# First down product: when the weight sums are formed and when the residual is read back

## The chip, the cores and the metric

The kernel runs on one core of a Trainium2 chip. The metric is the device time of one execution in microseconds (us), the median of several runs. The kernel's program is fixed at build time: each engine (PE for matmuls, ACT, DVE, POOL, and SP, which here only issues DMAs) has its own list of instructions, runs it strictly in order, and waits on semaphores where an operand or a buffer isn't ready. DMAs are issued by SP (plain loads and stores) and by POOL (transfers from memory to memory that can also add into their destination). Both kinds are carried by the same 16 DMA engines.

## The reference

One macaron layer on 512 tokens of width 1024, all in float32. The change touches only the end of the first of its three parts:

```
x = x + 0.5 * swiglu_ffn(rmsnorm(x, ffn1_norm), ffn1_w_gate, ffn1_w_up, ffn1_w_down)
x = x + hybrid_mixer(rmsnorm(x, mix_norm), ...)
x = x + 0.5 * swiglu_ffn(rmsnorm(x, ffn2_norm), ffn2_w_gate, ffn2_w_up, ffn2_w_down)
x = rmsnorm(x, final_norm)

swiglu_ffn(x, g, u, d) = (silu(x @ g) * (x @ u)) @ d      # g, u: 1024 x 2816, d: 2816 x 1024
```

## The kernel before

Each float32 product is made of three faster passes (`mm3`): an operand is split into a high part (rounded, ACT, `whi` for weights and `ah` for activations) and a low part (the remainder, DVE, `wlo`), and high x high, high x low and low x high are added up in PSUM. So each block of weights is loaded by a DMA into a tile `raw`, cast by ACT, subtracted by DVE, and only then multiplied.

Both feed-forward parts multiply by a Strassen-like scheme (Winograd's form, seven block products in place of eight). It needs sums of weight blocks. The gate and up weights are summed on DVE while they are in the chip. The sums of the four blocks of the down weights (B11, B12, B21, B22) are formed in memory: T1 = B11 + B12, T2 = T1 + B22, T3 = B12 + B22, T4 = T2 + B21 (signs are left to the other operand), each cut into G = 6 groups of rows (the last one half as wide), stored in DRAM tiles named `wsum`. For each of these 24 tiles there are two DMAs from POOL: one copies the first term into it, the other adds the second term to it (`accum_op`). These 48 steps are listed in `Down.steps`; those of one tile, and those that build on another tile, must land in order, and POOL waits for a landing where the next step reads or adds to the same tile.

The order in time of the first feed-forward part:

1. `ffn_up`, the up product, some 220 us. Its loop over blocks of 128 hidden columns (`for n in range(PLAIN, KF)`, 17 blocks, about 10 us each) fetches two blocks ahead (`fetch`, L436 and L437: two DMAs of 512 KB into one of two `raw` tiles), casts (`high` and `low`, L444 and L449), and multiplies. Once a block, and three times before the loop, it calls `down.make_sums(..., 2)`: POOL copies one column of a fresh tile (`mark`, L673, which ties POOL to that point of the program) and issues the next two of the 48 steps (L675). That is 20 calls, so 40 steps.
2. The first three of the seven products of the down part: for each of the six groups T2, B11 and T1 (`Down.product`: load L702 by `fetch`, cast and subtract L131 and L132 by `split`, then 12 matmuls, 6 for the last group). The block stands under `tc.manual_schedule(engines={SP})`: SP issues in the order in which the program is written. `product` issues one more step of the weight sums at every second product from the seventh on; that is where the last eight of the 48 go.
3. The other four products (T3 and B22 in turn, then B21, then T4). This block stands under the scheduler, which may move DMAs of SP ahead of others where it believes that they can start. From the 20th product on, each `product` also issues one of eight loads of the residual (`down.loads`, L760: 256 KB of the layer's input each, into the tiles `x`, which hold blocks of activations, `xa`, up to the end of the up product). The result is transposed and added to `x` (`add`, L835), and the second norm follows.

There are four `raw` tiles for the loads of the down part (two of the up product's and two of the weights' pool) and four pairs of tiles for their high and low parts, used in strict rotation. So SP can issue a load when the DVE is done with the load four products back, and the casts run at most four products ahead of PE.

Of the kernel before, what the change touches and what calls it, by code (L numbers as in the profile page):

```python
# [11 lines left out]
AF = mybir.ActivationFunctionType  # L12
ALU = mybir.AluOpType
# [3 lines left out]
P = 128  # L17
D = 1024
S = 512
KD = D // P  # L20
NT = S // P
FF = 2816
KF = FF // P
KH = KF // 2
# [15 lines left out]
PLAIN = 5  # L40
# [13 lines left out]
def layer(  # L54
# [31 lines left out]
    nc = tc.nc  # L86
# [14 lines left out]
    def name(what):  # L101
        n_tiles[0] += 1
        return f"{what}_{n_tiles[0]}"

    def temp(dtype=F32):
        return tpool.tile([P, S], dtype, tag="t", name=name("t"))

    def bank(tag="mm", bufs=4):
        return ps.tile([P, S], F32, tag=tag, name=name(tag), bufs=bufs)

    def abank():
        return bank("a", 4)
# [3 lines left out]
    B11, B12, B21, B22, T1, T2, T3, T4 = range(8)  # L116
    A11, S1, S3, S2, A12, A22, S4 = range(7)
# [4 lines left out]
    def piece(n=1):  # L122
        for _ in range(min(n, len(todo))):
            what, *args = todo.pop(0)
            what(*args)


    def split(src, hi, lo, scale=None):

        if scale is None:  # L130
            nc.scalar.copy(hi, src)  # L131
            nc.vector.tensor_tensor(lo, src, hi.bitcast(F32), op=ALU.subtract)  # L132
        else:
            nc.scalar.activation(hi, src, AF.Copy, scale=scale)
            nc.vector.scalar_tensor_tensor(
                lo, src, scale, hi.bitcast(F32), op0=ALU.mult, op1=ALU.subtract
            )
# [48 lines left out]
    def residual_tiles():  # L186
        pairs = [xpool.tile([P, 2 * S], F32, tag=f"x{k}", name=name("x")) for k in range(KD // 2)]
        return [pairs[k // 2][:, k % 2 * S : (k % 2 + 1) * S] for k in range(KD)]

    x = residual_tiles()  # L190
# [4 lines left out]
    ident = const.tile([P, P], F32, name="ident")  # L195
# [70 lines left out]
    class Norm:  # L266


        def __init__(self, which):
            self.which, self.h, self.acc = which, {}, None  # L270

        def add(self, k, square=True):
            hi = hpool.tile([P, S], F32R, tag="h", name=name("hhi"))
            lo = hpool.tile([P, S], F32R, tag="h", name=name("hlo"))
            split(x[k], hi, lo, gain_sb[:, self.which, k : k + 1])
            self.h[k] = hi, lo
            if square:
                self.square(k)
# [41 lines left out]
        def blocks(self, pool, aside):  # L320
# [43 lines left out]
            def extra():  # L364
                return pool.tile([P, 4 * HT], F32R, tag="extra", name=name("sa"), bufs=2)

            free = [3, 2, 1, 0]
            return [(scale, k) for k in range(KD)] + [
                (add, s1, a21, a22, ALU.subtract),
                (add, s2, s1, a11, ALU.add),  # L370
                (add, a21, a11, a21, ALU.add),
                (whole, S3, a21, by_x(free), -1.0),
                (whole, S2, s2, by_x(free), -1.0),
# [244 lines left out]
    G = len(groups)  # L618

    class Down:  # L620
# [11 lines left out]

        def __init__(self, order, pair, block):

            self.order, self.pair, self.block = order, pair, block

            self.terms = {T1: (B11, B12), T2: (T1, B22), T3: (B12, B22), T4: (T2, B21)}
            self.wsum = {  # L640
                (i, g): dram.tile(list(block(B11, g).shape), F32, name=name("wsum"))
                for i in self.terms for g in range(G)
            }

            self.steps = sorted(
                (g + at + 2 * (i - T1), at, i, g)
                for i in self.terms for g in range(G) for at in range(2)
            )
# [18 lines left out]

        def make_sums(self, after, n):

            part, self.steps[:n] = self.steps[:n], []  # L670
            with tc.manual_schedule(engines={mybir.EngineType.Pool}):
                mark = small.tile([P, 1], F32, tag="mark", name=name("mark"))
                nc.gpsimd.tensor_copy(mark, after[:, 0:1])  # L673
                for _, at, i, g in part:
                    nc.gpsimd.dma_start(  # L675
                        self.rows(i, g), self.rows(self.terms[i][at], g),
                        **(dict(accum_op=ALU.add) if at else {}),
                    )
# [86 lines left out]
    def whole(make):  # L765
        return [[(make(), 0, S)] for _ in range(2)]

    def scaled(dst, acc, scale, other, op=ALU.add):
        nc.vector.scalar_tensor_tensor(dst, acc, scale, other, op0=ALU.mult, op1=op)

    def halved(acc):
        z = [temp() for _ in range(2)]
        for tt in range(2):
            nc.scalar.activation(z[tt], acc[tt][0][0], AF.Copy, scale=0.5)
        return z


    n1, n2, n3 = Norm(0), Norm(1), Norm(2)
# [15 lines left out]

    KPS = (2, 3, 0, 1)
    order1 = [0, 1, KH, KH + 1] + [f + KH * j for f in range(2, KH) for j in range(2)]
    down1 = Down(order1, lambda f: (f % KH, f // KH), block1)
    down2 = Down(list(range(KF)), lambda f: (f // 2, f % 2), block2)

    with tc.tile_pool(name="act1", bufs=1, reuse_waits="tile") as apool:  # L800
        down1.begin(apool)
        ffn_up(n1, wA1, down1, loaded=False)
        p1, p5, p6 = whole(bank), whole(bank), whole(abank)

        with tc.manual_schedule(engines={mybir.EngineType.SP}):
            for g in range(G):
                down1.product(p6, g, S2, T2)
                down1.product(p1, g, A11, B11)
                down1.product(p5, g, S1, T1)
                if g == 0:  # L810

                    x[:] = residual_tiles()
                    down1.loads, down1.loads_from = [(x[k], xT[k]) for k in range(KD)], 19
        p7 = whole(abank)
        u2 = halved(p6)

        y = [down1.acts[i // 2][:, i % 2].rearrange("p k c -> p (k c)") for i in range(2 * NT)]
        down1.product(p7, 0, S3, T3)
        for tt in range(2):
            scaled(u2[tt], p1[tt][0][0], 0.5, u2[tt], ALU.subtract)  # L820
            scaled(y[NT + 2 + tt], p5[tt][0][0], 0.5, u2[tt])
        for g in range(G):
            if g + 1 < G:
                down1.product(p7, g + 1, S3, T3)
            down1.product(p5, g, S4, B22, further=True)

        def add(d):

            tp = bank() if d >= KD // 2 else abank()
            for t in range(NT):  # L830
                nc.tensor.transpose(
                    tp[:, t * P : (t + 1) * P],
                    y[d // 4 * NT + t][:, d % 4 * P : (d % 4 + 1) * P], ident,
                )
            nc.vector.tensor_tensor(x[d], x[d], tp, op=ALU.add)  # L835
            n2.add(d)

        for tt in range(2):
            todo.append((scaled, y[NT + tt], p5[tt][0][0], -0.5, u2[tt], ALU.subtract))
            todo.append((scaled, y[NT + 2 + tt], p7[tt][0][0], 0.5, y[NT + 2 + tt]))  # L840
        for g in range(G):
            down1.product(p1, g, A12, B21, further=True)
            piece()
        todo.extend((add, d) for d in range(KD // 2, KD))
        for tt in range(2):
            nc.scalar.activation(y[tt], p1[tt][0][0], AF.Copy, scale=0.5)
        ahead = down1.operands(0, A22, T4, -1.0)
        for g in range(G):
            a, w = ahead
            if g + 1 < G:  # L850
                ahead = down1.operands(g + 1, A22, T4, -1.0)
            down1.mms(p7, g, a, w, further=True)
            piece()
        for tt in range(2):
            scaled(y[2 + tt], p7[tt][0][0], -0.5, u2[tt], ALU.subtract)
        for d in range(KD // 2):
            add(d)
        rooms[:] = [(wpool, "raw", RAW, 1024)]

    with tc.tile_pool(name="mix", bufs=1, reuse_waits="tile") as mpool:  # L860
# [558 lines left out]
    with tc.tile_pool(name="act2", bufs=1, reuse_waits="tile") as apool:  # L1419
        down2.begin(apool)  # L1420

        for half in range(2):
            for t in range(NT):
                tp = abank()
# [76 lines left out]
        p1, p5, p6 = whole(bank), whole(bank), whole(abank)  # L1501
# [145 lines left out]
```

## Time and profile before

| | us |
|---|---|
| median of 3 runs | 867.18 |
| lowest and highest | 867.08, 868.5 |
| span of the profiled execution (first to last instruction) | 865.4 |
| median of the runs less that span | 1.8 |
| up product, POOL's steps of the weight sums | 38.6 to 230 |
| first three products of the down part, on PE | 231.7 to 278.6 |
| the other four, with the residual's additions | 278.6 to 352 |

The profiled execution's own time is known as its span alone; the timed runs lie 1.7 to 3.1 us above it. Times in the profile count from the span's first instruction. A row of the timeline or of the chain of work begins with its start and its length in us; `x2` behind it is a number of instructions merged into one row, and what stands in square brackets is how long the engine had been idle and who ended that. A matmul of 512 columns is drawn 0.39 us long, since matmuls overlap in the array; while nothing is late, the next one starts 0.22 to 0.23 us after it, and that distance is what a matmul costs.

### The profile page before, as it was taken

The page shows a single profiled execution, that of the slowest core. Times are in us where ns is not written, and L with a number is a line of the kernel's source. Part 1 is how long each engine was busy: PE and PEld are TensorE (multiplying, and loading weights), DVE is VectorE, ACT ScalarE, POOL GpSimd, SP SyncE. Part 2 cuts the span into 40 slices and gives each one's busy share as a digit, 9 for nine tenths or more (in the row PEclk, how much of TensorE's full clock was granted, in tenths as well). Part 3 has the DMA queues.
Part 4 walks back from the last instruction along what each step waited for, and adds up shares of the span by engine and source line. Part 5 has one row for each costly group of instructions (what it writes and reads, how often), then busy time and mean ns, then how long its engine had stood idle before and what let it go on. Part 6 is the DMA issues. An engine that isn't in the chain of part 4 may idle for free.

```text
span 865.4 us, 14127 instructions
## 1 busy us (share of the span) xinstructions
PE 849.9 (98%) x5296; PEld 755.9 (87%) x5296; DVE 708.1 (82%) x1115; ACT 500.9 (58%) x859; POOL 126.9 (15%) x204
## 2 busy tenths in 40 slices
PE   9999999999999999989999999999999999999996
PEld 7889999999987788867878788889999999988885
DVE  7999888898777868685878676969888898887896
ACT  7445555555556646548656756445555555566573
POOL 0113112211123000120011000102112111122000
PEclk9999999999999999999999999999999999999998
DMA  8168778778899763322212017257778778799832
GB/s 291 59 187 225 214 229 203 187 197 212 244 309 260 239 208 132 113 86 73 80 55 98 25 61 251 78 146 216 217 231 203 188 198 211 246 333 342 273 108 97
DMA packets 72244, 158.50 MB, mean 183 GB/s; under 512 B 6112, under 2 KB 29168, under 8 KB 71792
## 3 DMA queue, kind: packets, MB, share of 16 engines
q1 hardware_dynamic: 49088, 110.93, 36.7%
q0 software_dynamic: 22656, 46.14, 24.9%
q8 instruction: 41, 0.67, 0.3%
q10 hardware_dynamic: 432, 0.54, 0.2%
q14 instruction: 27, 0.22, 0.1%
HBM read 153.38 MB, written 50.34 MB: 235 GB/s over the span
## 4 chain that ended last, share of the span: by engine, by line
PE 89%; DMA 3%; DVE 3%; ACT 2%; issue 1%; SPq 0%; ACTq 0%; DVEq 0%
PE mm L176 21%; PE mm L177 21%; PE mm L178 21%; PE a L177 7%; PE a L178 7%; PE a L176 7%; DMA raw<-wsum 2%; PE a L1167 1%; DMA raw<-in_wB_dram 1%; PE a L1221 1%; PE a L1209 1%; DVE wlo L132 1%; DMA raw<-in_wA_dram 1%; DVE t L1088 1%; ACT prob L1148 1%
## 5 line engine op out<-in xcount | busy, mean ns | idle before, releaser
L132 DVE TENSOR_TENSOR wlo<-raw,whi 128x1024 fp32r<-128x1024 f32 (+2 forms) x115 | 125.3, 1096 | 28.7 <-ACT whi L131 28.4
L131 ACT CAST whi<-raw 128x1024 fp32r<-128x1024 f32 (+2 forms) x115 | 107.3, 944 | 67.8 <-PE mm L177 15.5
L177 PE MATMUL mm<-ha,whi 128*128 128x256 f32 x408 | 115.5, 283 | 0.0
L178 PE MATMUL mm<-ha,wlo 128*128 128x256 f32 x408 | 114.9, 282 | 0.0
L176 PE MATMUL mm<-ha,whi 128*128 128x256 f32 x408 | 114.9, 282 | 0.0
L540 ACT ACTIVATE t<-mm 128x256 f32<-128x256 f32 x102 | 39.3, 386 | 122.5 <-PE mm L178 121.9
L449 DVE TENSOR_TENSOR wlo<-wsum,whi 128x1024 fp32r<-128x1024 f32 x68 | 83.0, 1221 | 14.5 <-ACT whi L444 14.5
L178 PEld LDWEIGHTS mm<-ha,wlo 128*128 128x128 f32 x408 | 77.3, 189 | 0.0
L176 PEld LDWEIGHTS mm<-ha,whi 128*128 128x128 f32 x408 | 77.2, 189 | 0.1
L177 PEld LDWEIGHTS mm<-ha,whi 128*128 128x128 f32 x408 | 77.1, 189 | 0.1
L176 PE MATMUL mm<-hhi,whi 128*128 128x512 f32 x192 | 75.6, 396 | 0.3 <-ACT whi L131 0.2
L177 PE MATMUL mm<-hlo,whi 128*128 128x512 f32 x192 | 75.6, 394 | 0.0
L673 POOL COPY mark<-t 128x1 f32<-128x1 f32 x40 | 14.9, 373 | 409.1 <-DVE t L585 231.1
L178 PE MATMUL mm<-hhi,wlo 128*128 128x512 f32 x192 | 74.8, 391 | 0.0
L675 POOL DMA_DIRECT2D wsum<-in_wB_dram x72 | 70.2, 1086 | 13.2 <-issue 10.1
L444 ACT CAST whi<-wsum 128x1024 fp32r<-128x1024 f32 x68 | 67.9, 1049 | 4.1 <-PE mm L177 3.9
L177 PE MATMUL mm<-wlo,ah 128*128 128x512 f32 x176 | 68.9, 392 | 0.5 <-DVE wlo L132 0.5
L176 PE MATMUL mm<-whi,ah 128*128 128x512 f32 x176 | 68.5, 390 | 0.1
L178 PE MATMUL mm<-whi,ah 128*128 128x512 f32 x176 | 68.5, 389 | 0.0
L449 DVE TENSOR_TENSOR wlo<-raw,whi 128x512 fp32r<-128x512 f32 x68 | 62.3, 952 | 0.3 <-ACT whi L444 0.3
L444 ACT CAST whi<-raw 128x512 fp32r<-128x512 f32 x68 | 56.2, 826 | 8.3 <-PE mm L177 4.4
L177 PE MATMUL a<-wlo,ah 128*128 128x512 f32 (+1 forms) x154 | 55.7, 362 | 1.3 <-DVE wlo L132 1.3
(211 smaller groups left out, 2378.3 us busy)
## 6 DMA issues: line engine op xcount, KB each, us to landing
raw<-in_wA_dram SPq DMA_DIRECT2D x87, 512.0 KB, 5.2
wsum<-in_wB_dram POOLq DMA_DIRECT2D x60, 512.0 KB, 7.2
raw<-wsum SPq DMA_DIRECT2D x40, 512.0 KB, 6.1
raw<-in_wB_dram SPq DMA_DIRECT2D x30, 512.0 KB, 5.7
wsum<-wsum POOLq DMA_DIRECT2D x20, 512.0 KB, 5.4
x<-in_xT_dram SPq DMA_DIRECT2D x16, 256.0 KB, 7.3
raw<-in_wQK_dram SPq DMA_DIRECT2D x8, 512.0 KB, 3.6
raw<-in_wO_dram SPq DMA_DIRECT2D x8, 512.0 KB, 3.4
```

Source lines behind the costliest of these rows:

```text
L131: nc.scalar.copy(hi, src)
L132: nc.vector.tensor_tensor(lo, src, hi.bitcast(F32), op=ALU.subtract)
L176: nc.tensor.matmul(acc, a[0], b[0], start=start, stop=False, **more)
L177: nc.tensor.matmul(acc, a[0], b[1], start=False, stop=False, **more)
L178: nc.tensor.matmul(acc, a[1], b[0], start=False, stop=stop, **more)
L444: nc.scalar.copy(hi, src)
L449: nc.vector.tensor_tensor(lo, src, hi.bitcast(F32), op=ALU.subtract)
L540: nc.scalar.activation(dst, src, AF.Copy, scale=scale)
L673: nc.gpsimd.tensor_copy(mark, after[:, 0:1])
L675: nc.gpsimd.dma_start(self.rows(i, g), self.rows(self.terms[i][at], g), **(dict(accum_op=ALU.add) if at else {}),)
L1088: nc.vector.tensor_tensor(q3, q3, rs[:, t, :].unsqueeze(2).to_broadcast([P, 8, HD]), op=ALU.mult)
L1148: nc.scalar.activation(p, p, AF.Copy, scale=rt)
```

## The change

It has two parts.

- `make_sums` takes its number of steps from a list, `rates`, as long as that has entries: four steps in each of the three calls ahead of the loop, three in each of the next six calls, two in each of the next nine. That is 12 + 18 + 18 = 48 steps in 18 calls. The last two calls of the up product issue only their `mark`, and `Down.product` finds no step left, so its eight marks and eight DMAs in the down part are gone. Down part two has no list and stays as it was.
- The block of the last four products of the first down part now also stands under `tc.manual_schedule(engines={SP})`. The order of PE's and DVE's instructions is the same as before; on ACT two neighbouring casts trade places at one point. On SP the eight loads of the residual move from among the loads of the first three products to where the program issues them.

SP at the start of the first down product, before (L702: weights of the down part, L760: the residual; `wsum_12` and the like are tiles of weight sums, `in_wB1` is a block of the weights themselves):

```order
L702 DMA raw_462_2750<-wsum_12_115 128x1024
L760 DMA x_502_3036<-in_xT_dram 128x512
L702 DMA raw_480_2882<-in_wB1_dram 128x4x256
L702 DMA raw_481_2884<-wsum_6_109 128x1024
L702 DMA raw_507_3044<-wsum_13_116 128x1024
L760 DMA x_501_3035<-in_xT_dram 128x512 x2
L702 DMA raw_512_3067<-in_wB1_dram 128x4x256
L760 DMA x_502_3036<-in_xT_dram 128x512
L760 DMA x_503_3037<-in_xT_dram 128x512
L702 DMA raw_517_3089<-wsum_7_110 128x1024
```

The same place now (L704 is the line that was L702):

```order
L704 DMA raw_462_2762<-wsum_12_115 128x1024
L704 DMA raw_480_2892<-in_wB1_dram 128x4x256
L704 DMA raw_481_2894<-wsum_6_109 128x1024
L704 DMA raw_507_3052<-wsum_13_116 128x1024
L704 DMA raw_512_3075<-in_wB1_dram 128x4x256
L704 DMA raw_517_3097<-wsum_7_110 128x1024
```

The residual's loads are gone from here. They now stand on SP among the loads of T3 (`wsum_19` and following) and B22, one behind each:

```order
L704 DMA raw_591_3409<-wsum_19_122 128x1024
L762 DMA x_501_3043<-in_xT_dram 128x512
L704 DMA raw_596_3432<-in_wB1_dram 128x4x256
L762 DMA x_501_3043<-in_xT_dram 128x512
L704 DMA raw_601_3455<-wsum_20_123 128x1024
L762 DMA x_502_3044<-in_xT_dram 128x512
L704 DMA raw_606_3478<-in_wB1_dram 128x4x256
L762 DMA x_502_3044<-in_xT_dram 128x512
```

Eight more rows of that kind follow; the last load of the residual is issued behind the load of the fourth group of B22.

POOL in the second to fourth call of `make_sums`, before (`512x1x256` is a step that reads the weights, `16x8192` one that copies a finished sum):

```order
L673 COPY mark_146_600<-t_145_592 128x1
L675 DMA wsum_6_109<-in_wB1_dram 512x1x256
L675 DMA wsum_8_111<-in_wB1_dram 512x1x256
L673 COPY mark_180_726<-t_179_720 128x1
L675 DMA wsum_12_115<-wsum_6_109 16x8192
L675 DMA wsum_7_110<-in_wB1_dram 512x1x256
L673 COPY mark_197_812<-t_187_739 128x1
L675 DMA wsum_9_112<-in_wB1_dram 512x1x256
L675 DMA wsum_13_116<-wsum_7_110 16x8192
```

The same calls now:

```order
L675 COPY mark_146_602<-t_145_594 128x1
L677 DMA wsum_12_115<-wsum_6_109 16x8192
L677 DMA wsum_7_110<-in_wB1_dram 512x1x256
L677 DMA wsum_9_112<-in_wB1_dram 512x1x256
L677 DMA wsum_13_116<-wsum_7_110 16x8192
L675 COPY mark_180_730<-t_179_724 128x1
L677 DMA wsum_8_111<-in_wB1_dram 512x1x256
L677 DMA wsum_12_115<-in_wB1_dram 512x1x256
L677 DMA wsum_10_113<-in_wB1_dram 512x1x256
L677 DMA wsum_14_117<-wsum_8_111 16x8192
L675 COPY mark_197_818<-t_187_745 128x1
L677 DMA wsum_18_121<-in_wB1_dram 512x1x256
```

Twice as many steps stand behind a mark, and a step and the one that builds on it (`wsum_7` and then `wsum_13<-wsum_7`) now fall into the same call, so POOL waits for a landing within it.

The diff, without the lines that are only indented:

```diff
-        def __init__(self, order, pair, block):
+        def __init__(self, order, pair, block, rates=()):
             self.order, self.pair, self.block = order, pair, block
+            self.rates = list(rates)
...
         def make_sums(self, after, n):
+            n = self.rates.pop(0) if self.rates else n
             part, self.steps[:n] = self.steps[:n], []
...
-    down1 = Down(order1, lambda f: (f % KH, f // KH), block1)
+    down1 = Down(
+        order1, lambda f: (f % KH, f // KH), block1, [4] * (PLAIN - 2) + [3] * 6 + [2] * 9
+    )
...
-        p7 = whole(abank)
-        u2 = halved(p6)
+        with tc.manual_schedule(engines={mybir.EngineType.SP}):
+            p7 = whole(abank)
+            u2 = halved(p6)
...
```

Everything from `p7 = whole(abank)` to the last `add(d)` of the first down part is indented under the new `with`, and otherwise unchanged.

More of the change, by code (lines that the diff above doesn't have):

```diff
@@ L813, in layer @@
                     down1.loads, down1.loads_from = [(x[k], xT[k]) for k in range(KD)], 19
-        p7 = whole(abank)
-        u2 = halved(p6)
[L817 to L857, printed above, removed]
+        with tc.manual_schedule(engines={mybir.EngineType.SP}):
+            p7 = whole(abank)
+            u2 = halved(p6)
+            y = [down1.acts[i // 2][:, i % 2].rearrange("p k c -> p (k c)") for i in range(2 * NT)]
+            down1.product(p7, 0, S3, T3)
+            for tt in range(2):
+                scaled(u2[tt], p1[tt][0][0], 0.5, u2[tt], ALU.subtract)
+                scaled(y[NT + 2 + tt], p5[tt][0][0], 0.5, u2[tt])
+            for g in range(G):
+                if g + 1 < G:
+                    down1.product(p7, g + 1, S3, T3)
+                down1.product(p5, g, S4, B22, further=True)
+            def add(d):
+                tp = bank() if d >= KD // 2 else abank()
+                for t in range(NT):
+                    nc.tensor.transpose(
+                        tp[:, t * P : (t + 1) * P],
+                        y[d // 4 * NT + t][:, d % 4 * P : (d % 4 + 1) * P], ident,
+                    )
+                nc.vector.tensor_tensor(x[d], x[d], tp, op=ALU.add)
+                n2.add(d)
+            for tt in range(2):
+                todo.append((scaled, y[NT + tt], p5[tt][0][0], -0.5, u2[tt], ALU.subtract))
+                todo.append((scaled, y[NT + 2 + tt], p7[tt][0][0], 0.5, y[NT + 2 + tt]))
+            for g in range(G):
+                down1.product(p1, g, A12, B21, further=True)
+                piece()
+            todo.extend((add, d) for d in range(KD // 2, KD))
+            for tt in range(2):
+                nc.scalar.activation(y[tt], p1[tt][0][0], AF.Copy, scale=0.5)
+            ahead = down1.operands(0, A22, T4, -1.0)
+            for g in range(G):
+                a, w = ahead
+                if g + 1 < G:
+                    ahead = down1.operands(g + 1, A22, T4, -1.0)
+                down1.mms(p7, g, a, w, further=True)
+                piece()
+            for tt in range(2):
+                scaled(y[2 + tt], p7[tt][0][0], -0.5, u2[tt], ALU.subtract)
+            for d in range(KD // 2):
+                add(d)
```

## The prediction

> **What bounds the kernel now.** I read the page first, then busy time by stage, then the chain of waits where PE lost time, then landings by line.
>
> ```profile
> PE 849.9 (98%) x5296; PEld 755.9 (87%) x5296; DVE 708.1 (82%) x1115; ACT 500.9 (58%) x859; POOL 126.9 (15%) x204
> DMA  8168778778899763322212017257778778799832
> ```
>
> PE is the bound, so only time that PE waits is worth anything. DMA is full (8, 9, 9, 9) in slices 10 to 13, 216 to 303 us, where both parts of the change end. By stage (PE busy and count, PEld, DVE, ACT, POOL, clock, DMA share, GB/s):
>
> ```profile
> 72.00:130.00 58.00, 58.00 (x491) 58.00 (x490) 51.25 (x73) 31.58 (x59) 11.20 (x19) 1.00 0.80 221
> 232.00:259.00 27.00, 27.00 (x121) 22.28 (x119) 21.27 (x29) 15.84 (x22) 6.22 (x6) 1.00 1.05 325
> 259.00:284.00 25.00, 23.15 (x95) 16.98 (x93) 19.28 (x28) 15.34 (x25) 8.56 (x10) 1.00 1.05 270
> 284.00:309.00 25.00, 25.00 (x112) 20.69 (x111) 20.19 (x25) 17.11 (x25) 0.00 (x0) 1.00 0.69 216
> ```
>
> The same matmuls fill rows three and four, each 25 us: 112 start where DMA is at 0.69, only 95 where it is at 1.05. The 17 missing ones, at 25 / 112 = 0.22 us, are **3.8 us** of lost PE time. The up product loses nothing, nor do 232 to 259 us. The losses one by one:
>
> ```profile
> 258.77 0.39 PE L178 MATMUL a<-whi,ah 128*128 128x512 f32 x1
> 258.99 0.39 PE L176 MATMUL mm<-whi,ah 128*128 128x512 f32 x1
> 259.65 0.50 PE L177 MATMUL mm<-wlo,ah 128*128 128x512 f32 x1 [0.27 <-DVE wlo L132]
> ...
> 275.24 0.49 PE L176 MATMUL mm<-whi,ah 128*128 128x512 f32 x1
> 275.97 0.50 PE L177 MATMUL mm<-wlo,ah 128*128 128x512 f32 x1 [0.23 <-DVE wlo L132]
> ...
> 278.64 0.49 PE L176 MATMUL a<-whi,ah 128*128 128x512 f32 x1
> 279.90 0.50 PE L177 MATMUL a<-wlo,ah 128*128 128x512 f32 x1 [0.77 <-DVE wlo L132]
> ...
> 282.53 0.39 PE L176 MATMUL a<-whi,ah 128*128 128x512 f32 x1
> 283.43 0.50 PE L177 MATMUL a<-wlo,ah 128*128 128x512 f32 x1 [0.52 <-DVE wlo L132]
> ```
>
> Starts in step are 0.22 apart (258.77, 258.99); these four gaps of 0.66, 0.73, 1.26 and 0.90 make 2.7 us of the 3.8; the rest follows right behind them in smaller pieces. Who was late is in the chain:
>
> ```profile
> 247.28 9.91 DMA raw<-in_wB_dram
> 257.28 1.06 ACT whi L131
> 258.37 1.24 DVE wlo L132
> ...
> 269.80 7.64 DMA raw<-wsum
> 277.54 1.06 ACT whi L131
> 278.62 0.51 DVE wlo L132
> ...
> 279.76 0.75 DVE t L769 x2
> ...
> 282.24 1.14 DVE wlo L132
> ```
>
> Loads of 512 KB take 9.9 and 7.6 us to land, then cast, subtraction, PE. Only the last gap has another link: the low part of T3's second group stands behind four DVE operations on the finished products (279.76 to 282.24). Next, what a load takes there: line L702 between 224 and 245 us (the residual's loads about it), between 246 and 284 (weight sums about it), and between 285 and 330 (neither):
>
> ```profile
> DMA to landing us min/median/max: 6.0/6.4/7.3
> ```
>
> ```profile
> DMA to landing us min/median/max: 6.5/7.9/11.8
> ```
>
> ```profile
> DMA to landing us min/median/max: 2.4/3.9/4.6
> ```
>
> Four buffers at 2.7 us a product (12 x 0.227) give 10.9 us from one load into a buffer to the next; less cast (1.05), subtraction (1.22) and some 0.3 of handing over, about 8.3 us remain for the landing. The first and third row fit under that, the second doesn't. Traffic in 246 to 284 us by queue (q0 POOL's, q1 SP's):
>
> ```profile
> q0 software_dynamic: 3228, 3.41, 53.6%
> q1 hardware_dynamic: 3874, 6.62, 51.1%
> ```
>
> The eight late steps are 3.41 MB and take as much of the DMA engines as all loads together.
>
> **The change part by part.** *Eight steps out of the down product.* Takes q0's 53.6% out of 246 to 284 us. Loads then land as in the third row, up to 7.3 us at worst with the residual beside them, under 8.3; the waits on DMA go: the first three gaps and their followers. The fourth I don't count whole. T3's low part would be early, but that of its second group still stands behind the four DVE operations, and two of those wait for the last of the three products, which PE ends as it enters T3. From there: two operations (1.3 us), the subtraction (1.22), some 0.3 of handing over, 2.8 us; PE wants it one product (2.7) and one matmul (0.23) later. It is just in time or 0.3 us late. Gain 3.8 - 0.3 = **3.5 us**; ends: 1.9 (last two gaps stay with what follows them) and 3.8.
>
> *Eight steps more in the up product*: six more in the three calls ahead of the loop, six more in the loop's first six, four fewer in its last two. Up there PE never waits, so the price is what a fetch comes too late by:
>
> ```profile
> 75.66 0.55 SPq L437 DMA_DIRECT2D raw<-in_wA_dram  x1
> ```
>
> ```profile
> 84.03 0.62 ACT L444 CAST whi<-raw 128x512 fp32r<-128x512 f32 x1
> 85.23 0.39 ACT L540 ACTIVATE t<-a 128x256 f32<-128x256 f32 x1 [0.58 <-PE a L178]
> ```
>
> The cast could take the tile 8.4 us after the issue, and ACT idles 0.58 us behind it, so 9.0 us cost PE nothing; beyond that, us for us. Landings of L437 in 72 to 214 us, and in 36 to 72 us, where the steps run into it:
>
> ```profile
> DMA to landing us min/median/max: 4.5/5.7/6.8
> ```
>
> ```profile
> DMA to landing us min/median/max: 8.0/8.2/8.3
> ```
>
> How a step delays a fetch: q0, the only traffic from 84 to 88 us with two fetches issued at 85.25 and 85.63 (adding steps), and q0 from 42.6 to 45 us (plain steps, two fetches issued there too):
>
> ```profile
> q0 software_dynamic: 743, 0.74, 117.8%
> ```
>
> ```profile
> q0 software_dynamic: 207, 0.78, 90.6%
> ```
>
> Adding steps run at 0.74 MB in 4 us, 2.8 us for 512 KB, plain ones at 0.78 MB in 2.4 us, 1.6 us; and meanwhile the fetches moved nothing: a load stands behind the steps issued before it. A third adding step in a block thus puts up to 2.8 us on 5.7: 8.5 us, under 9.0. That is the worst of the six calls of three; where the third is a copy, it is less. Closest is the fetch at 75.3 us: the call just ahead of the loop and the first in it now hold seven steps together, four adding (11.3 us) and three plain (4.8 us), from 67 us on; with the fetch's own 1 MB (3.2 us at the 325 GB/s of 232 to 259 us) that ends at 86.3, 2.3 over the cast, 1.7 over what is free. If some of the fetch passes in between, nothing. Between these I take **0.5 us** lost in all, nearer to nothing since SP's loads and steps issued together did share elsewhere (8.2 us at most of the 9.0, in the row from 36 to 72); ends 0 and 6 (each of the six fetches 1 us over).
>
> The Trainium skill's page "DMA: Bandwidth & Descriptors", section "Queues, rings and completion order", says that each DMA engine goes round its queues packet by packet. By that a fetch's 3.2 us of transfer could at most double, 5.7 + 3.2 = 8.9 us to land, the up product would lose nothing and the sum be -3.5. The trace from 84 to 88 us doesn't agree: one queue had it all.
>
> *POOL's waits within a call* and its marks: behind a waiting step stands only the next mark. A mark holds the tile that it reads:
>
> ```profile
> DVE t L589 <- POOL mark L673: 0.4, 1, 0.4
> ```
>
> That is one wait of DVE on a mark, 0.4 us. Eight tiles at three a block come round after 2.7 blocks, 26 us; a landing that POOL waits for within a call is far shorter (loads beside steps took 8.3 at most), so nothing. The eight dropped marks ran on a POOL with nothing else to do: nothing.
>
> *The residual's loads later.* In front of the loads of the down part they cost SP a wait and issue time:
>
> ```profile
> SPq L760 <- PE a L178: 9.5, 1, 9.5
> SPq L702 <- DVE wlo L132: 35.3, 18, 3.9
> L760 SPq DMA_DIRECT2D x<-in_xT_dram x8: 327/432/1262, 224.7 to 240.3; - x8
> ```
>
> The 9.5 us held up the loads that PE needed from 232 us on, and it lost nothing up to 259, so their removal is worth nothing by itself. In the new place, 271 to 293 us, the tiles are long free; eight issues at 0.43 us lie in SP's waits for DVE (35.3 us in 18). Their 2 MB stand beside eight loads, 4 MB, over 22 us: 290 GB/s, less than the 325 at which 232 to 259 us lost nothing. Cost 0; ends 0 and 0.8 (each load at 0.1 us of delay). They are read from here on, 35 us later:
>
> ```profile
> L835 DVE TENSOR_TENSOR x<-x,mm x4: 680/684/689, 328.9 to 339.0; 128x512 f32<-128x512 f32 x4
> ```
>
> **Sum**: -3.5 + 0.5 = -3.0 us. The profiled span of 865.4 becomes 862.4; the median of the runs lies 1.8 us above the span, so 864.2, against 867.18.
>
> **The rivals.**
> 1. *Slower: the up product runs short of DMA.* With three steps a block, some 7 us of steps and 3.2 us of fetch fill a block of 10 us. For it: share 0.80 already, and the row of 84 to 88. Against: PE has 9.0 us free at each fetch, and copies and half-size steps fill three of the six calls. It decides once the six fetches land at 9.9 us each: 0.9 x 6 = 5.4 us, the gain of 3.5 and the bound for slower. At 10 us each: 867.18 - 3.5 + 6 = 869.7. The page named above, section "Issuing engines are not separate DMA queues", has all queues on the same 16 engines; by that the work isn't removed but moved, which is this rival's premise. The trace agrees: 53.6% and 51.1% add up to over 1 there.
> 2. *The gain is half.* The last two gaps stay because DVE's order or the residual's new place holds them: 867.18 - 1.9 = 865.3. For it: the chain's link at 279.76. Against: 1.26 of it followed a landing at 277.4.
> 3. *No change.* Rival 1 in part, 3 us, or loads that are slow for their small pieces and not for company: 867. Against: 3.9 us for the same loads from 285 us on.
>
> **How the numbers follow.** Forecast 0.60 (863.4 to 865.4), rival 1 0.11, rival 2 0.13, rival 3 0.11, a larger gain from waits further down 0.05. Within 0.2% (1.7 us, what a measurement here can tell) lie rival 3 and half of rival 2: 0.17; slower 0.11; faster 0.72. The range leaves out rival 1 and the ends beyond: 862.9 (all 3.8 and half a us) to 866.8.
>
> **What would show it.** In the changed profile: no traffic of q0 after some 220 us; L704 landing at 4 us up to 271 us and under 8 beside the residual; PE's starts 0.23 apart from 232 to 284; L437 landing at 7 to 9 us between 72 and 130 with ACT waiting on DMA for less than 1 us. I am wrong if PE waits in the up product (its blocks longer than 10 us), or if a gap of over 0.5 us stays at 279 to 284.

## The result, and the profile after

The changed kernel takes 865.56 us (median of 8 runs, 864.84 to 867.41) against 867.44 us (8 runs, 867.08 to 869.66): a ratio of 0.9974, 95% interval 0.9964 to 0.9984. It is 1.9 us faster, where 3.0 were forecast. The profiled span falls by 2.2 us, from 865.4 to 863.2. By the number alone, 865.56 lies nearest to rival 2's 865.3; which account holds has to be read from the rows.

The DMA row of the 40 slices, changed kernel:

```profile
DMA  8199998877576764322212026248778778899832
```

Counted from 0, slices 10 to 13 (216 to 303 us) read 8, 9, 9, 7 before (the prediction took the last for a 9) and read 5, 7, 6, 7 now; slices 2 to 5 (43 to 130 us) read 6, 8, 7, 7 and now 9, 9, 9, 9. The traffic has moved forward. By stage (us, PE busy and count, PEld, DVE, ACT, POOL, clock, DMA share, GB/s), the same stretches as before:

```profile
72.00:130.00 58.00, 56.94 (x478) 56.53 (x477) 50.99 (x72) 30.99 (x57) 17.70 (x25) 1.00 1.06 283
...
259.00:284.00 25.00, 25.00 (x112) 20.70 (x111) 19.70 (x28) 15.16 (x24) 0.00 (x0) 1.00 0.65 209
```

The second row has its 112 matmuls again, where 95 started before: the whole 3.8 us are back. The first has lost 13 of its 491, at 0.118 us each 1.5 us. PE's starts around the two places of that loss (start, duration, engine, line, operation, tiles, shape; in brackets idle time and who ended it):

```profile
86.46 0.28 PE L178 MATMUL mm<-xa,wlo 128*128 128x256 f32 x1
87.45 0.39 PE L176 MATMUL a<-ha,whi 128*128 128x256 f32 x1 [0.71 <-ACT t L540]
87.68 0.29 PE L177 MATMUL a<-ha,whi 128*128 128x256 f32 x1
...
107.32 0.28 PE L178 MATMUL mm<-xa,wlo 128*128 128x256 f32 x1
107.95 0.39 PE L176 MATMUL a<-ha,whi 128*128 128x256 f32 x1 [0.35 <-ACT t L540]
108.18 0.28 PE L177 MATMUL a<-ha,whi 128*128 128x256 f32 x1
```

In step, starts lie 0.12 apart. 0.99 and 0.23 are 0.98 too much, 0.63 and 0.23 are 0.62 too much: **1.6 us**. From here on "lost" means this sum, the distance of PE's starts beyond 0.118 us (256 columns) or 0.227 us (512). The chain of waits says who was late:

```profile
75.86 10.56 DMA raw<-in_wA_dram
86.54 0.48 issue
87.03 0.39 ACT t L540
87.45 0.39 PE a L176
...
96.74 10.18 DMA raw<-in_wA_dram
```

Two fetches of the up product's weights took 10.6 and 10.2 us to land; ACT's cast waited for them, ACT's copy of a finished product (L540) stood behind the cast, and PE waited for the bank that the copy frees. -3.8 + 1.6 = -2.2 us, the difference of the spans; the other stages differ by 0.2 us at most, with both signs.

### The profile page after: what moved, and what is told of

The parts are those of the page before. It is cut to its first block, busy times and chain, and to the rows that moved or that the text cites. A ratio compares the mean times of both kernels' runs of the same rounds, so it can differ in the third digit from the quotient of the medians.

```text
span 863.2 us, 14110 instructions
## 1 busy us (share of the span) xinstructions
PE 848.8 (98%) x5296; PEld 757.5 (88%) x5296; DVE 708.3 (82%) x1115; ACT 501.1 (58%) x859; POOL 120.1 (14%) x196
## 4 chain that ended last, share of the span: by engine, by line
PE 91%; DVE 3%; DMA 2%; ACT 2%; issue 1%; SPq 0%; ACTq 0%; DVEq 0%
PE mm L176 22%; PE mm L177 21%; PE mm L178 21%; PE a L176 7%; PE a L177 7%; PE a L178 7%; DMA raw<-in_wA_dram 2%; PE a L1172 1%; PE a L1226 1%; PE a L1214 1%; DVE t L1093 1%; DVE wlo L449 1%; ACT prob L1153 1%; PE a L211 0%; PE a L1431 0%
## 5 line engine op out<-in xcount | busy, mean ns | idle before, releaser
L131 ACT CAST whi<-raw 128x1024 fp32r<-128x1024 f32 (+2 forms) x115 | 106.9, 944 | 57.7 <-PE mm L177 15.5
L540 ACT ACTIVATE t<-mm 128x256 f32<-128x256 f32 x102 | 39.2, 384 | 121.5 <-PE mm L178 120.8
L132 DVE TENSOR_TENSOR ah<-acts,ah 128x512 fp32r<-128x512 f32 (+1 forms) x72 | 45.7, 641 | 14.5 <-ACT ah L131 14.2
```

What stands on the lines that cost most here:

```text
L540: nc.scalar.activation(dst, src, AF.Copy, scale=scale)
```

## The experiments

Each ran beside the kernel before on the same chip, in three groups (e1 to e4; e0 and e5 to e7; e8 to e10); ratios are to that, whose medians there were 867.99, 868.89 and 867.78 us. The last two columns are PE's losses in one profiled execution each.

| kernel | median us | ratio, 95% interval | span | lost 28 to 232 us | lost 232 to 330 us |
|---|---|---|---|---|---|
| before | 867.44 | | 865.4 | 0 | 3.9 |
| changed | 865.56 | 0.9974 [0.9964, 0.9984] | 863.2 | 1.6 | 0.2 |
| e1 late steps only | 865.55 | 0.9975 [0.9959, 0.9992] | 864.8 | 3.2 | 0.1 |
| e2 order only | 865.17 | 0.9968 [0.9952, 0.9985] | 863.6 | 0 | 2.2 |
| e3 19 even calls | 864.03 | 0.9956 [0.9944, 0.9967] | 862.3 | 0 | 0.8 |
| e4 calls earlier | 874.08 | 1.0066 [1.0046, 1.0087] | 872.5 | 10.7 | 0 |
| e0 changed, again | 865.8 | 0.9961 [0.9948, 0.9975] | 863.9 | 2.7 | 0.1 |
| e5 18 even calls | 864.56 | 0.9950 [0.9937, 0.9963] | 862.8 | 0.7 | 0.2 |
| e6 sixth call lighter | 864.9 | 0.9960 [0.9948, 0.9972] | 863.2 | 0.9 | 0.2 |
| e7 plain twice | 872.1 | 1.0033 [1.0018, 1.0048] | 872.7 | 10.9 | 0 |
| e8 18 calls, light first | 865.06 | 0.9973 [0.9961, 0.9984] | 864.4 | 1.8 | 0.1 |
| e9 even, old order | 864.12 | 0.9965 [0.9951, 0.9979] | 862.4 | 0.6 | 0.2 |
| e10 plain once | 864.87 | 0.9970 [0.9958, 0.9981] | 862.2 | 0.5 | 0.2 |

### e1 and e2: one part of the change alone

e1 is the kernel before with the list of rates, the residual's loads where they were:

```diff
...
-    down1 = Down(order1, lambda f: (f % KH, f // KH), block1)
+    down1 = Down(order1, lambda f: (f % KH, f // KH), block1, [4] * (PLAIN - 2) + [3] * 6 + [2] * 9)
```

> All 48 steps in the up product as in the changed kernel, but the residual's loads where they were before, among the loads of the first three products. Theory A (the late steps took the DMA engines and held up the down part's loads; the residual's place does not matter): the first down product loses 0 to 0.5 us of PE time, the up product 1.6 us as in the changed kernel, span 863.2 to 863.8 us, ratio 0.997 to 0.998. Theory B (the residual's loads among the first loads started the lateness, steps only added to it): 1.5 to 3.8 us stay lost in the down product, span 864.7 to 867.0.

e2 is the changed kernel without that list, with the order held on SP:

```diff
     down1 = Down(
-        order1, lambda f: (f % KH, f // KH), block1, [4] * (PLAIN - 2) + [3] * 6 + [2] * 9
+        order1, lambda f: (f % KH, f // KH), block1
     )
```

> The residual's loads in program order as in the changed kernel, but two steps a call and eight steps in the down product as before. The up product loses nothing. Theory A: the down product loses 2 to 3.8 us, since the steps are there and 2 MB of residual come on top of the last of them, span 863.6 to 865.4, ratio 0.998 to 1.000. Theory B: it loses under 1 us, span 861.6 to 862.6, ratio about 0.996.

By stage, e1:

```profile
72.00:130.00 58.00, 55.75 (x466) 55.07 (x465) 48.79 (x69) 31.09 (x58) 17.48 (x25) 1.00 1.07 289
259.00:284.00 25.00, 25.00 (x112) 20.72 (x111) 19.71 (x28) 16.00 (x25) 0.00 (x0) 1.00 0.54 168
```

and e2, where PE waits at 283.2 and 289.8 us for the low part of a weight:

```profile
259.00:284.00 25.00, 24.35 (x108) 19.85 (x107) 15.97 (x23) 11.76 (x19) 7.45 (x10) 1.00 1.15 281
284.00:309.00 25.00, 24.41 (x106) 19.52 (x105) 20.52 (x28) 17.76 (x26) 0.00 (x0) 1.00 0.91 293
```

Taking the late steps away is enough for the down product: in e1 all 112 matmuls start there although the residual's loads are where they were. But the residual's place isn't worthless while the late steps run: e2 loses 2.2 us instead of 3.9. The two gains overlap; they don't add up. And the price in the up product belongs to the rates alone: e2 loses nothing there, e1 3.2 us, twice what was expected of it.

### e0, e3, e5, e8: how the 48 steps are spread

By the rates of adding steps 2.8 us, plain ones 1.6 and copies 1.3 (half of it for the last group), the calls of the change hold up to 8.5 us of steps. Three other lists, each in the place of `[4] * (PLAIN - 2) + [3] * 6 + [2] * 9`: e3, 19 calls of at most 5.7 us; e5, 18 calls of at most 6.0; e8, 18 calls, light at first, then up to 7.2:

```diff
+        [2, 2, 2, 3, 2, 3, 3, 2, 2, 4, 2, 3, 2, 2, 3, 3, 2, 3, 3]    (e3)
+        [3, 3, 3, 2, 3, 3, 2, 2, 4, 2, 3, 2, 2, 3, 3, 2, 3, 3]       (e5)
+        [2, 2, 2, 3, 2, 3, 3, 2, 3, 3, 3, 3, 3, 2, 3, 3, 3, 3]       (e8)
```

> The changed kernel with its 48 steps dealt out over 19 calls by what they cost (adding step 2.8 us of DMA, plain copy from the weights 1.6, copy of a sum 1.3, half for the last group), so that no call holds more than 5.7 us. Theory A1 (PE's 1.6 us in the up product come from single calls whose steps hold the DMA engines past the next fetch): no fetch lands over 9 us after its issue, the up product loses 0 to 0.2 us, span 861.6 to 861.9, ratio 0.9955. Rival (it is the number of steps in the up product as a whole): about 1.6 us stay lost, span 863.2, ratio 0.9974.

> The changed kernel once more, unaltered, beside the next three on the same chip. Every theory: its own result again, 0.9974 of the kernel before, with some 1.6 us of PE's waits in the up product (87.5 and 108 us) and none in the down product.

> All 48 steps in 18 calls with at most 6.0 us of steps in one, the last of them at about 209 us instead of the 220 us of the partition in 19. Theory A (a call of over about 7 us of steps makes the fetch behind it late; steps that still run when the first loads of the down product are fetched make those late): no PE loss in the up product and none at 235 us, where the 19-call partition lost 0.6 us; span about 861.6 us. Rival (the 0.6 us at 235 us are not the last steps'): 862.3 us as with 19 calls. Rival (earlier steps cost the up product in any case, and the 19 calls were lucky): 1 to 3 us of waits between 70 and 130 us, span 863 to 865.

> The changed kernel with the 48 steps in 18 calls, light at first (3.2, 4.4, 4.1 us) and up to 7.2 us after that, the last at about 209 us. Theory A3: the first calls no longer meet the traffic of the up product's start (no 0.7 us near 77 us, which the 18 even calls had), the last do not reach into the down product (no 0.6 us at 235 us, which the 19 had); the calls of 6.9 and 7.2 us cost at most 0.4 us each; span 861.6 to 862.4. Rival (6.9 to 7.2 us in one call is already too much): 1 to 2.5 us lost between 125 and 205 us, span 862.6 to 864.

e3 by stage:

```profile
72.00:130.00 58.00, 58.00 (x491) 58.00 (x491) 51.34 (x73) 31.57 (x59) 14.56 (x21) 1.00 0.96 243
232.00:259.00 27.00, 26.66 (x118) 21.69 (x117) 25.34 (x35) 20.63 (x28) 0.00 (x0) 1.00 0.72 229
259.00:284.00 25.00, 25.00 (x112) 20.71 (x111) 19.71 (x27) 15.12 (x23) 0.00 (x0) 1.00 0.65 207
```

All of the steps are issued in the up product, at a DMA share of 0.96 from 72 to 130 us, and PE loses nothing there: it isn't the amount that cost the changed kernel its 1.6 us but how much is queued when a single fetch is issued. The 0.6 us that e3 loses instead, at 235 us, are in its chain:

```profile
224.93 7.89 DMA raw<-in_wB_dram
...
232.89 1.06 ACT whi L131
...
233.98 1.24 DVE wlo L132
...
235.26 0.50 PE mm L177
```

The nineteenth call is issued at 220 us and its adding steps land at 230 and 232, beside the first loads of the down product. In e5 the last call lies at 209 us, and this loss is gone (232 to 330 us: 0.2). It has 0.7 us at 77 us in its place, where the third call is heavier than e3's; half of what was expected came. In e8 the rival held: the first calls cost nothing, but two fetches, behind the calls of 6.2 and 7.2 us, were late again (its calls of 6.4 and, twice, of 6.9 us made none late, so the sum of a call doesn't settle it alone):

```profile
145.97 10.30 DMA raw<-in_wA_dram
...
166.58 10.61 DMA raw<-in_wA_dram
```

e3 has the lowest median (864.03 us, 863.21 to 864.39 in 10 runs); e1 and e2 on the same chip had medians of 865.55 and 865.17. It beats the kernel before by 0.44%, and the changed one, which did not run beside it, by 1.5 us of median. By the ratio to the kernel before, e5 is level with it (0.9950 against 0.9956, intervals that overlap). e5 beside e0 on one chip is 1.2 us faster (864.56 against 865.8, ranges that overlap). e0 also shows what a single profiled execution is good for: the same kernel lost 1.6 us in one and 2.7 in the other, since a third fetch (issued at 116.69, landing after 10.52 us) was late. Differences of about 1 us between the losses of two kernels in the table can be of that kind.

### e9: the even calls with the old order

```diff
...
-    down1 = Down(order1, lambda f: (f % KH, f // KH), block1)
+    down1 = Down(order1, lambda f: (f % KH, f // KH), block1, [3, 3, 3, 2, 3, 3, 2, 2, 4, 2, 3, 2, 2, 3, 3, 2, 3, 3])
```

> The kernel before (residual's reloads where the scheduler put them, no order held on SP) with the 48 steps in 18 even calls. Theory A (late steps alone cost the down product; the order of SP's loads is worth nothing once they are early): as with the order held, no loss of over 0.3 us in the down product, about 0.7 us in the up product, span 862.8. Rival B (the residual's loads cost something of their own when they go ahead of T3's loads): 0.5 to 2 us of PE's waits between 275 and 291 us, span 863.3 to 864.8.

By stage:

```profile
72.00:130.00 58.00, 57.62 (x486) 57.42 (x486) 51.13 (x72) 30.93 (x57) 14.42 (x22) 1.00 0.98 247
259.00:284.00 25.00, 25.00 (x112) 20.69 (x111) 19.71 (x27) 15.35 (x23) 0.00 (x0) 1.00 0.56 168
```

Theory A: no loss in the down product, a span of 862.4 us (e5: 862.8). With the late steps gone, the order held on SP shows no gain: e9 and e5, which differ in it alone, lose 0.8 and 0.9 us in all (one profile each, on two chips).

### e6, e7, e10: what makes a fetch late

e6 moves one adding step from the sixth call to the seventh:

```diff
-        [4] * (PLAIN - 2) + [3] * 6 + [2] * 9
+        [4] * 3 + [3, 3, 2, 4, 3, 3] + [2] * 9
```

> The changed kernel with one adding step (A30) taken from the sixth call, near 91 us, to the seventh, near 102 us: the sixth has 5.6 us of steps instead of 8.4, the seventh 7.0 instead of 4.2, of which one step adds and three do not. Theory A1 (adding steps that follow one another on the queue hold the DMA engines, so the price is by the adding steps in one call): the 0.6 us near 108 us go and nothing comes in their place, the 0.97 us near 87.5 stay; span about 862.6. Theory A2 (any bytes of steps ahead of a fetch delay it alike): the loss near 108 us goes, and one of about the same size comes near 118 us, behind the seventh call; span about 863.2.

e7 issues two plain DMAs for each adding one, e10 only the first of them (the lines that set `plain` and make the tiles `twice` are left out; e10 hasn't the last two lines):

```diff
                     nc.gpsimd.dma_start(
                         self.rows(i, g), self.rows(self.terms[i][at], g),
-                        **(dict(accum_op=ALU.add) if at else {}),
+                        **(dict(accum_op=ALU.add) if at and not self.plain else {}),
                     )
+                    if at and self.plain:
+                        nc.gpsimd.dma_start(self.twice[i, g], self.rows(self.terms[i][at], g))
```

> In the first down product's sums each adding DMA is replaced by two plain ones of the same bytes (one into the sum's place, one into a tensor that nobody reads), so the second weights are not added and the first part's down product is of wrong weights; all counts, calls and places of the changed kernel stay, and the DMA engines' time by the rows is about equal (2 x 1.6 us for the 2.8 us of an adding step). Theory A1 (adding is what shuts the fetches out): the fetches issued near 76 and 97 us land in 7 to 9 us, no PE loss in the up product, span about 861.6. Theory A2 (the bytes do it): they land in 10 us or more and PE loses 1 to 3 us there as in the changed kernel, span 863 to 865.

> The changed kernel, with one plain DMA in the place of each adding one in the first down product's sums: the second weights are not added, so the first part's down product is of wrong weights; the counts, calls and places are the changed kernel's. The traffic of the steps falls from some 7 to 8.5 us a call to about 5. Theory A3 (it is the DMA time of the steps ahead of a fetch that makes it late, adding or not; two plain DMAs for each adding one made the fetches of 76 and 101 us land 13 us after issue): the fetches land in 5 to 8 us, PE loses nothing in the up product and nothing at the down product's start, span about 861.4. Theory A4 (the number of DMAs, or the wait of one call for the next, does it): the fetch near 76 us lands in about 10 us again, PE loses 1 us or more, span 862.5 or more.

The late fetches in the chains of e6, e7 and e10:

```profile
75.95 10.01 DMA raw<-in_wA_dram
...
116.31 9.99 DMA raw<-in_wA_dram
```

```profile
76.10 13.26 DMA raw<-in_wA_dram
...
101.06 12.84 DMA raw<-in_wA_dram
```

```profile
76.12 10.03 DMA raw<-in_wA_dram
```

In e6 the loss near 108 us is gone, as both theories had it, and theory A2's loss near 118 us, behind the seventh call, didn't come. The 0.4 us at 127 us stand behind the eighth call, which is the changed kernel's own; e0 lost 0.9 us at the same place, so they are no price of the step that was moved. By e6 alone A1 would stand. e7 decides it: without an adding step the fetches land later than in the changed kernel, not sooner, and PE waits 3.4 and 3.0 us for them. Adding is not what makes a fetch late; A1 falls. The size is beyond theory A2 too (10.9 us lost, a span of 872.7 us; what follows such a wait is told with the hardware), and e7 isn't quite equal to the changed kernel in what is queued: POOL's wait for a landing in the third call ended at 72.1 us, not at 75.1, so ten DMAs issued from 66.6 us on stood ahead of the fetch at 76.10, where the changed kernel had four. What the queues did meanwhile (packets, MB, share of the 16 engines; q0 is POOL's, q1 SP's), from 84 to 88 us in the changed kernel, from 82 to 88 in e7, with fetches under way in both:

```profile
q0 software_dynamic: 702, 0.70, 112.4%
q1 hardware_dynamic: 48, 0.08, 7.3%
```

```profile
q0 software_dynamic: 408, 1.49, 66.5%
q1 hardware_dynamic: 337, 0.75, 33.9%
```

By these rows fetches stand still beside adding steps (7.3% of the engines' time) and get a third beside plain ones. From 100 to 104 us, again in the changed kernel and then in e7, and again with two fetches under way in both, it is the other way round; in e7 q1 has no row there:

```profile
q0 software_dynamic: 379, 0.38, 58.5%
q1 hardware_dynamic: 270, 0.78, 54.7%
```

```profile
q0 software_dynamic: 358, 1.31, 100.3%
```

So the kind of step doesn't tell whether a fetch moves. In both kernels a fetch moves nothing at first (in the changed one from 75.9 to some 78 us and from 96.7 to some 100, in e7 from 76.1 to some 80 and from 101.1 to some 104.5), and shares the engines with the steps after that. The Trainium skill's page "DMA: Bandwidth & Descriptors", section "Queues, rings and completion order", has each DMA engine go round its queues packet by packet; the stretches of sharing fit that, those in which only one queue moves don't. What ends such a stretch isn't shown.

What goes with a late landing is how much is queued. Of the second loads (the line of L437) whose landing the traces give, between 60 and 215 us in all kernels but e2 and e4, those that landed within 7 us found steps that were all down at most 6 us after the load's issue. Those that took 10 us or more found steps that needed 9 to 14 us, or else had more steps issued right behind them (near 75 us).

e10, with one plain DMA where e7 has two, was expected to have no late fetch (A3). It has one, of 10.0 us, and 0.5 us of loss, between A3's nothing and A4's 1 us; the other fetches of that line landed in 5.0 to 8.6 us. Here is POOL:

```profile
71.94 0.51 POOL L677 DMA_DIRECT2D wsum<-wsum  x1 [3.10 <-DMA wsum<-in_wB_dram]
...
72.55 2.21 POOL L677 DMA_DIRECT2D wsum<-in_wB_dram  x3
```

Its fourth step of the third call waits for a landing within the call, until 71.94, and the fourth call follows at once: seven steps ahead of the fetch at 76.12. Nothing shows that a shorter call would have been free there, so A4, the wait of one call against the next, isn't excluded for this fetch; for the rest A3 stands.

### e4: the calls 3 us earlier in each block

```diff
                 copy(u[:, HT:], acc, -1.0)
+                if early:
+                    down.make_sums(u[:, HT:], 2)
                 sum24(n + 1)
                 product(up_hi, cut(w24, S, S), A22, False)
                 nc.vector.tensor_tensor(u[:, HT:], up_hi, u[:, HT:], op=ALU.add)
-                down.make_sums(u[:, HT:], 2)
+                if not early:
+                    down.make_sums(u[:, HT:], 2)
```

(`early = down is down1`.)

> The changed kernel with its own rates, but in the first part's loop each call stands ahead of the addition to u, some 3 us earlier in a block of 10 us, so that a call's steps have 3 us more before the next fetch. Theory A1: the heavy calls end before or soon after the fetch is issued, its landing goes from over 10 us to 7 to 8, the up product loses 0 to 0.3 us, span 861.6 to 861.9. Rival (a mark ahead of the addition makes DVE wait for a POOL that waits for a landing): DVE waits on marks for several us in all, and PE loses 1 us or more, span over 862.6.

Waits between 60 and 130 us (engine, line, waited for; us in total, times, longest):

```profile
POOL wsum L681 <- DMA wsum<-in_wB_dram: 15.4, 3, 7.3
DVE t L588 <- POOL mark L679: 7.3, 1, 7.3
...
PE a L178 <- DVE wlo L449: 5.3, 1, 5.3
```

The mark now reads a tile that DVE goes on to add to, so DVE waits for POOL, and POOL stands in a wait for a landing (7.3 us). DVE is held for as long, and PE behind it 5.3 us. The rival held, and theory A1 failed in its own terms too: two fetches, issued at 82.75 and 104.19 us, landed after 11.1 and 11.6 us, not 7 to 8. The slow start after PE's wait is below, with the hardware.

## Why the prediction was right or wrong

*Right: faster, for the reason given.* The late steps shared the DMA engines with the down product's loads; gone, L704 lands in time. Lines L704 from 246 to 284 us and q1's traffic there:

```profile
DMA to landing us min/median/max: 2.5/4.4/5.9
```

```profile
q1 hardware_dynamic: 4783, 8.37, 69.1%
```

The forecast was some 4 us, and under 8 beside the residual; q0 has no row there any more. e1 and e9 show that this part alone does it.

*The gain: forecast 3.5, measured 3.8.* The 0.3 us kept back for T3's second group didn't come:

```profile
278.19 1.28 DVE L771 SCALAR_TENSOR_TENSOR acts<-mm,t 128x512 f32<-128x512 f32 x2
279.38 4.62 DVE L132 TENSOR_TENSOR wlo<-raw,whi 128x1024 fp32r<-128x1024 f32 x4
```

The four DVE operations (two are ahead of these rows, from 276.99) run without a wait between them and end by 279.4; the subtraction behind them is the group's low part, done by about 280.6 (279.38 + 1.22), where PE's second group starts at 281.1 (its 112 starts are in step). Rival 2, half the gain, is out with it.

*The step that failed: 0.5 us lost in the up product, by fetches that come late.* It cost 1.6 us (2.7 in the repeat), and by the prediction's own sign ("I am wrong if PE waits in the up product") it failed: L437 landed in 8.7 to 10.6 us between 72 and 130 us, where 7 to 9 were forecast. Two of its numbers were wrong, against each other.

First, "9.0 us cost PE nothing" is 9.6. I stopped at ACT's idle time before L540; but PE had spare time behind that copy. In the kernel before, L540 starts at 85.23 and ends at 85.62, and PE takes the bank only here:

```profile
86.38 0.28 PE L176 MATMUL a<-ha,whi 128*128 128x256 f32 x1
```

About 0.7 us more. Landing minus loss bears it out: 10.56 - 0.98 and 10.18 - 0.62 in the changed kernel, 10.48 - 0.90, 10.44 - 0.89 and 10.52 - 0.91 in e0, 10.29 - 0.66 and 10.57 - 0.97 in e1, 10.01 - 0.42 and 9.99 - 0.38 in e6, 10.30 - 0.71 and 10.61 - 1.05 in e8, 10.03 - 0.45 in e10: 9.55 to 9.63 each time. Beyond 9.6 us it is us for us, as the prediction said. (The fetch at 67 us has 8.6 us: e1's landed after 10.06 us there and cost 1.42.)

Second, the landings. For the fetch at 75.3 us the working had 86.3 with seven steps ahead of it in order, and it landed at 86.42. That the two agree is luck. POOL waited in the third call for a landing, and the last three of the seven steps were issued only behind the fetch (75.86 us):

```profile
75.11 0.52 POOL L677 DMA_DIRECT2D wsum<-wsum  x1 [5.58 <-DMA wsum<-in_wB_dram]
...
76.03 3.12 POOL L677 DMA_DIRECT2D wsum<-in_wB_dram  x3
```

The last two of these landed at 88.0 and 92.4 us, behind the fetch; the order of issue wasn't kept, and the working had left out the fetch that was issued at 66.4 us beside the first of the steps (q1 moved 1.04 MB from 66 to 72 us). I had then discounted the 86.3 towards nothing because loads had shared the engines elsewhere. Here the fetch shared them too, once it moved, and was late all the same. And "up to 2.8 us on 5.7: 8.5 us" for a third adding step failed for the fetch at 96.74: 10.2. POOL shows why 5.7 was no base for it:

```profile
88.28 0.52 POOL L677 DMA_DIRECT2D wsum<-wsum  x1 [7.13 <-DMA wsum<-in_wB_dram]
88.79 0.76 POOL L677 DMA_DIRECT2D wsum<-in_wB_dram  x1
...
91.38 3.52 POOL L677 DMA_DIRECT2D wsum<-in_wB_dram  x3 [0.30 <-issue]
```

The fifth call was held up 7.1 us by a landing within it, and its last two steps went out at 88.3 and 88.8, just ahead of the sixth call's three adding ones. Five steps in a row, 11.3 us by the prices above, not three. The step ahead of them landed at 93.5; 93.5 + 11.3 + 3.2 for the fetch itself is 108.0, and the last of these landed at 108.5, the fetch ahead of it at 106.9. So taking nothing for POOL's waits within a call failed too. Nobody waited for POOL (the wait for a mark stayed 0.4 us), but the steps behind the wait were bunched. That the bunching, and not the third step alone, made this fetch late is read from the rows, and e6 fits either: with one step fewer in the sixth call, and a wait of 6.4 us ahead of it, the fetch landed in 8.6 us. It wasn't tested by itself.

*The residual's loads: "their removal is worth nothing by itself".* True once the late steps are gone (e1, e9), but not for the reason given. With the late steps still there the new place saves 1.7 us (e2). That PE lost nothing up to 259 us didn't show that they cost nothing later. In the new place they cost nothing, as forecast; line L762 there:

```profile
DMA to landing us min/median/max: 4.0/5.7/7.2
```

*Rival 1, the up product short of DMA*, was the right fear, at a quarter of its size. Its point was six fetches at 9.9 us; with 9.6 us free, two of six came over it (three in e0). e7, with 13.3 and 12.8 us, is that rival in full: slower than before by 0.33%, the low clock behind its waits included. Rival 3, no change, is outside the interval (0.9964 to 0.9984). The sum, -3.0 by forecast, is -3.8 + 1.6 = -2.2 in the spans; 864.2 became 865.56.

## What to carry to other kernels

Work that is moved off a full stretch of DMA is paid for where it lands, and there what is queued when a single load is issued decides, not the sum: in the up product the same 48 transfers cost 1.6 to 3.2 us in clumps and 0 to 0.7 us in even calls. Find a load's slack by following it to the engine that is the bound, past every in-order neighbour, and compare it with all that is queued around the load, counting what an earlier wait on that queue has held back. And two changes that relieve the same stretch are not added up: one of them was enough here.

## What the runs showed of the hardware

An adding DMA from DRAM to DRAM went in packets of 1 KB (702 packets, 0.70 MB), a plain one in packets of 3.7 KB (358 packets, 1.31 MB), and by the rates above takes 2.8 us for 512 KB where the plain one takes 1.6. A load of SP's that is issued while several of either kind are queued by POOL moved nothing for some 2 to 4 us in these stretches, and shared the engines after that (54.7% against 58.5%); rows above.

In these runs PE paid twice for a wait of 3.0 us or more. e4 behind its wait of 5.3 us, by stretches (PE busy and count second, clock after the five engines):

```profile
80.00:81.00 1.00, 1.00 (x6) 1.00 (x6) 1.00 (x2) 0.45 (x1) 0.29 (x1) 0.50 0.83 288
...
87.00:90.00 3.00, 3.00 (x28) 3.00 (x27) 1.51 (x2) 2.44 (x4) 1.27 (x2) 1.00 1.11 322
```

The granted clock is 0.50, and matmuls of 256 columns start 0.21 us apart instead of 0.118, from 79.2 to about 85.1 us: some 28 starts, 2.6 us lost behind a wait of 5.3. In e7 the same followed waits of 3.4 us (until about 93.3, 3 us long) and 3.0 us (until about 120.7, 6 us long). Behind a wait of 1.7 us in e4 the granted clock stayed at 1.00, and behind the waits of 0.4 to 1.2 us in the other kernels only the first start was 0.1 us late. The Trainium skill's page "TensorE: Matmul & The Clock Gate", section "Part 1: The HAM clock gate (the "warmup" mystery)", has the clock halved after an idle window of about 3.4 us, in windows that run freely. The clock of 0.50 and the varying length agree; a wait of 3.0 us was enough here.
